# A two-layer hybrid backbone: quadrant sums of FFN weights by accumulating DMA, a plain last FFN part in the first layer, output by tokens

## The chip, the cores and the metric

One NeuronCore of a Trainium2 chip runs the whole program. The metric is device time in microseconds (us), the median of three runs. TensorE is PE in the profile, VectorE DVE, ScalarE ACT, GpSimd POOL, and SP is the engine that issues DMAs.

## What is computed

`x` is 512 latent tokens of width 1024, `ctx` 256 context tokens; all is float32, and there are two layers (`l` = 0 and 1 in the code, "first" and "second layer" here).

```python
hx = modulate(rmsnorm(x, norm1), sh1, sc1)            # shifts, scales, gates from c @ w_mod
... = split_proj(hx @ w_in)                           # 4 head groups: attention, HGRN2, GQA, Fourier
x = x + g1 * (concat(mixers) @ w_out)
x = x + g2 * swiglu(modulate(rmsnorm(x, norm2), sh2, sc2), w_ffn_in, w_ffn_out)
# swiglu(h): gate, up = split(h @ w_ffn_in); (silu(gate) * up) @ w_ffn_out, hidden width 2816
# the context does the same in the first layer only; at the end: rmsnorm(x, final_norm)
```

## The kernel before

**Float32 by halves.** Each float32 operand of a large product is split into two float16 parts, a high one and what is left (`cpo` makes the high part, mostly on ACT; `tto` or `sto` the low part, mostly on DVE), and each product is three matmuls (`PASS`). A weight tile is 128 partitions x 8 x 256.

**Two ways through a tile.** Of the feed-forward network (FFN) a layer has 22 weight tiles of the first product ("I") and 12 of the second ("F": 4 column blocks `p` times 3 parts `c` of the hidden width; the last part, `c` = 2, is shorter: 384 elements where the others have 512). A tile is done plainly, or by Winograd's form of Strassen's scheme (`fast`): the weight and the activations are cut in quadrants, and 7 products replace 8. For the 512 latent tokens that is 84 matmuls of 256 columns instead of 96 (63 instead of 72 in the last part); for the context, 84 of 128 columns instead of 48 of 256. `TUNE['cl']` lists the I tiles that are done plainly: 0, 1, 19 in the first layer, twelve in the second. All F tiles are fast but one, the last of the second layer.

**What a fast tile costs beside PE.** `split_fast` loads the tile in two halves (512 KB each, queue of SP), and makes seven operands of 512 elements a partition: the quadrants A11, A12, A22 and the sums S1 to S4. Each of the seven is a float16 copy with scale (ACT, `L418`) and a low part (DVE, `L434`); each of the four sums is one float32 TENSOR_TENSOR before that (`tto`, `L430`, DVE unless POOL is chosen). S2 is made from S1, S4 from S2. A plain tile has four such element passes over 1024 and no sums (`split_thread`). `pair_ev` puts the gate and up products together out of the seven results, `hid_pair` splits the hidden activations and forms their sums, and `resid_pair` adds a fast F tile's results to the residual (8 DVE instructions for latents, 8 for the context); their plain counterparts are `ffn_ev` and `resid_ffn` (2 DVE instructions for each group of 256 tokens).

**The order of the work** is fixed when the kernel is built: `Plan.run` takes operations from many threads, with a cost for each (`c_dve`, `c_act`, `c_pe`, a landing time `ldma` for a DMA), and appends each to its engine's queue. The queues then run in that order on the chip. Where the plan leaves a gap of over 1.2 us on PE, `fill` puts matmuls on constant data into it (`warm`, `L2466`, 256 columns each); they compute nothing that is used.

**The layer border and the end.** When a group's residual of the last F part is done, `norm_thread` starts: squares, sums over the partitions by a matmul with ones (`L799`), the power -1/2 on POOL (`L817`), a matmul that spreads the result (`L820`), then the modulated activations, which the next layer's first product (`L2054`) needs. At the very end the same thread multiplies the final gain in and writes the output with channels on the partitions; the host transposes it.

Of the kernel before, what the change touches and what calls it, by code (L numbers as in the profile page):

```python
# [2599 lines left out]
```

## Time and profile before

| | us |
|---|---|
| median of 3 runs (1721.33 to 1722.03) | 1721.76 |
| the profiled execution, its own time | 1725.08 |
| its span, first to last instruction | 1723.1 |
| PE busy | 1647.6 |
| DVE busy | 1486.0 |
| ACT busy | 980.8 |
| POOL busy | 150.7 |

The span in stages: input norm and modulation to 95 us, projections and mixers of the first layer to 495, its FFN to 1001, the layer border to 1011, projections and mixers of the second layer to 1321, its FFN to 1708, the final norm to 1723. A matmul's end is modelled and matmuls overlap, so PE busy says where PE stood still, not how fast it ran. Fill matmuls count as busy.

### The profile page before, as it was taken

To read this page: it belongs to the slowest core of one execution; us is meant where nothing else is said; L and a number is where in the kernel's file an instruction comes from. 1 tells how busy PE (TensorE), PEld (TensorE's weight loads), DVE (VectorE), ACT (ScalarE), POOL (GpSimd) and SP (SyncE) were. 2 spreads that over 40 slices of the span, in tenths; PEclk is the share of its full clock that TensorE was granted. 3 is DMA by queue.
4 is the path that set the end of the run, shared out by engine and by line. 5 is a ranking of instruction groups with operands and counts; after the bars stand their busy time and mean duration, and the time that the engine had idled before them with its cause. 6 is when DMAs were issued, how large, how long until landed. Compare 5 with 4: busy or idle time off the path is not lost.

```text
span 1723.1 us, 45511 instructions
## 1 busy us (share of the span) xinstructions
PE 1647.6 (96%) x19493; PEld 1425.4 (83%) x19493; DVE 1486.0 (86%) x3141; ACT 980.8 (57%) x1766; POOL 150.7 (9%) x179
## 2 busy tenths in 40 slices
PE   8999998999999999999999999899889999999998
PEld 5678877887888788898889888788778888888886
DVE  6879899898579897899889998999997788888897
ACT  5637885565465553355435483678955545465454
POOL 0212111230000000000000003430010000000000
PEclk9999999999999999999999999999999999999999
DMA  9822111245045654522352350001113333452631
GB/s 376 326 82 81 57 45 52 71 149 199 38 134 173 199 157 135 161 75 63 118 186 73 122 175 29 14 27 50 51 51 123 136 99 99 137 182 74 194 113 50
DMA packets 62859, 201.40 MB, mean 117 GB/s; under 512 B 6849, under 2 KB 9153, under 8 KB 62657
## 3 DMA queue, kind: packets, MB, share of 16 engines
q1 hardware_dynamic: 62656, 198.50, 35.1%
q8 instruction: 152, 2.49, 0.6%
q14 instruction: 51, 0.41, 0.1%
HBM read 178.55 MB, written 19.92 MB: 115 GB/s over the span
## 4 chain that ended last, share of the span: by engine, by line
PE 52%; DVE 34%; ACT 7%; DMA 4%; issue 2%; POOL 1%; SPq 1%; DVEq 0%; ACTq 0%; POOLq 0%
PE ps L2208 14%; DVE g L430 11%; PE ps L2049 10%; PE ps L2054 6%; DVE g L434 6%; PE ps L2168 5%; DMA g<-xsc 4%; PE ps L616 2%; PE ps L2272 2%; ACT g L418 2%; DVE pl L430 2%; PE ps L1218 2%; ACT g L416 1%; PE ps L1158 1%; PE ps L2466 1%
## 5 line engine op out<-in xcount | busy, mean ns | idle before, releaser
L430 DVE TENSOR_TENSOR g<-g,g 128x512 f32<-128x512 f32 (+7 forms) x698 | 441.0, 659 | 44.8 <-ACT g L416 32.3
L418 ACT ACTIVATE g<-g 128x512 f16<-128x512 f32 (+2 forms) x391 | 242.0, 644 | 236.2 <-DVE g L430 230.4
L2208 PE MATMUL ps<-g,g 128*128 128x256 f16 (+1 forms) x4032 | 361.9, 251 | 1.0 <-DVE g L434 0.8
L2208 PEld LDWEIGHTS <-g 128*128 128x128 f16 x4032 | 326.0, 98 | 40.1 <-issue 11.3
L434 DVE SCALAR_TENSOR_TENSOR g<-g,g 128x512 f16<-128x512 f32 (+4 forms) x442 | 301.1, 697 | 59.1 <-ACT g L418 56.0
L2049 PE MATMUL ps<-g,g 128*128 128x256 f16 x2256 | 271.8, 272 | 2.2 <-DVE g L434 2.0
L2272 PEld LDWEIGHTS <-g 128*128 128x128 f16 x2709 | 225.7, 98 | 43.0 <-issue 14.5
L2049 PEld LDWEIGHTS <-g 128*128 128x128 f16 x2256 | 218.0, 98 | 29.6 <-DVE g L434 2.5
L2272 PE MATMUL ps<-g,g 128*128 128x256 f16 (+1 forms) x1917 | 212.2, 269 | 15.3 <-DVE g L999 4.7
L416 ACT CAST g<-g 128x512 f16<-128x512 f32 (+3 forms) x269 | 162.9, 616 | 76.1 <-DVE g L430 46.6
L2054 PE MATMUL ps<-g,g 128*128 128x256 f16 x1632 | 201.9, 277 | 2.8 <-issue 1.4
L2054 PEld LDWEIGHTS <-g 128*128 128x128 f16 x1632 | 158.5, 99 | 36.8 <-issue 13.9
L2168 PE MATMUL ps<-g,g 128*128 128x256 f16 x1584 | 175.7, 273 | 0.0
L2168 PEld LDWEIGHTS <-g 128*128 128x128 f16 x1584 | 154.7, 98 | 18.9 <-issue 0.8
L416 ACT COPY g<-ps 128x512 f32<-128x512 f32 (+4 forms) x163 | 94.0, 583 | 119.4 <-PE ps L820 24.1
L1198 ACT ACTIVATE g<-ps 128x512 f32<-128x512 f32 x156 | 91.5, 595 | 31.9 <-PE ps L1232 23.1
L430 DVE TENSOR_TENSOR pl<-g,ph 128x512 f16<-128x512 f32 x137 | 93.2, 695 | 7.0 <-ACT ph L416 6.6
L430 DVE TENSOR_TENSOR g<-g 128x256 f32<-128x256 f32 (+3 forms) x197 | 89.4, 462 | 2.4 <-ACT g L754 1.8
L430 POOL TENSOR_TENSOR g<-g,g 128x256 f16<-128x256 f32 (+4 forms) x17 | 23.5, 1386 | 692.0 <-ACT g L416 575.9
L416 ACT CAST ph<-g 128x512 f16<-128x512 f32 (+2 forms) x141 | 80.5, 573 | 4.7 <-DVE g L430 1.0
L1582 ACT ACTIVATE g<-g 128x512 f32<-128x512 f32 x80 | 47.1, 637 | 41.5 <-DVE g L1550 41.3
L1218 PEld LDWEIGHTS <-ph 128*128 128x128 f16 x1248 | 63.3, 97 | 6.5 <-issue 1.7
(248 smaller groups left out, 2207.9 us busy)
## 6 DMA issues: line engine op xcount, KB each, us to landing
g<-in_wall_dram SPq DMA_DIRECT2D x180, 512.0 KB, 4.5
g<-in_wmod_dram SPq DMA_DIRECT2D x96, 512.0 KB, 6.2
g<-xsc SPq DMA_DIRECT2D x40, 256.0 KB, 5.3
xsc<-g SPq DMA_DIRECT2D x40, 256.0 KB, 3.0
g<-in_xg_dram SPq DMA_DIRECT2D x12, 512.0 KB, 6.9
g<-in_wall_dram SPq DMA_DIRECT2D x16, 384.0 KB, 3.3
xsc<-g SPq DMA_DIRECT2D x10, 512.0 KB, 3.1
g<-xsc SPq DMA_DIRECT2D x10, 512.0 KB, 4.5
```

The costliest lines, as they stand in the source:

```text
L416: S.copy(o, i)
L418: S.activation(out=o, in_=i, func=AF.Copy, scale=scale)
L430: return either(r, w, ("dve", c_dve(n), lambda: V.tensor_tensor(**f()), bias, True), ("pool", c_pool(n), lambda: G.tensor_tensor(**f()), 0 ...
L434: return vop(c_dve(n), r, w, lambda: V.scalar_tensor_tensor(**f()), True)
L1198: yield aop(c_act(512), [k], [k + (0,)], lambda pp=pp, bank=bank: S.activation(out=pp, in_=bank, func=AF.Exp, scale=scale), "exp")
L1218: T.matmul(bank[:, u, t, :], lhsT=a[:, i, q], rhs=v[:, b, :], start=(n == 0), stop=(n == 6 * nk - 1))
L1582: yield aop(c_act(512), prev, [k + (r,)], lambda R=R, r=r: S.activation(out=level_view(E, h)[:, :, :, r, :], in_=level_view(R, h)[:, :, :, ...
L2049: T.matmul(bank[:, cb, :], lhsT=W[a][:, kw, 128 * cb:128 * cb + 128], rhs=xh[b][:, kx, :], start=(first and n == 0), stop=(last and n == 2 ...
L2054: T.matmul(bank[:, t, :], lhsT=xh[b][:, k, 128 * t:128 * t + 128], rhs=wt[a][:, k, :], start=(first and n == 0), stop=(last and n == 2), s ...
L2168: T.matmul(bank[:, cb, :], lhsT=wt[a][:, k % 4, :], rhs=xh[b][:, k % 4, :], start=(k == 0 and n == 0), stop=(k == 7 and n == 2), skip_grou ...
L2208: T.matmul(into[name], lhsT=wt[:, y, kk, :], rhs=x[:, z, kk, :], start=(name in ("P1", "P6") and kk == 0 and n == 0), stop=(kk == 3 and n ...
L2272: T.matmul(o, lhsT=wt[:, y, j % 4, :], rhs=x[:, z], start=(name in ("P1", "P6") and j == js[0] and n == 0), stop=(j == js[-1] and n == 2), ...
```

## The change

1. **Sums by DMA.** The FFN weights lie in DRAM by quadrants (`wffn`), and the signs of the scheme are turned so that all four weight sums are additions. S1 and S3 are made by POOL-issued DMAs that add a 256 KB quadrant from DRAM onto one that was loaded (`acc`), two for each fast tile; S2 and S4 stay TENSOR_TENSORs, in place. The plan charges POOL `acp` = 0.9 us for one, lets the sum be there `acl` = 5.2 us later, and adds `accd` = 1.78 us to the DMA queue's clock. Low parts, residual and hidden sums carry the turned sign (`modN`, `-IWS`, subtractions); in `hid_pair` one TENSOR_TENSOR of two rows becomes two of one row.
2. **Which tiles.** First layer: I tile 19 becomes fast, and the four F tiles of `c` = 2 become plain, for latents and context (`PLAIN0`, `hid_pair`, `p_ffn_out`, `out_order`), latents first, group by group. Second layer: nine plain I tiles instead of twelve.
3. **Modulation.** The second layer's 12 modulation loads (2 MB each) begin with tile 16 instead of 14, and one comes with every second weight tile.
4. **Output.** `out_thread` replaces the last norm: PE transposes the gained activations, and the row scale goes in on the way out of PSUM (`L869`), so the output is written by tokens. After the last product, no fill matmuls are placed (`unwarm`).

```diff
-TUNE = {... 'm1': 14, ... 'cl': ((0, 1, 19), (0, 1, 2, 3, 4, 6, 8, 10, 12, 14, 16, 18)), ...}
+TUNE = {... 'm1': 16, ... 'acp': 0.9, 'acl': 5.2, 'gat': 1, 'whq': 16, 'pr_sp': 11, 'rr': 3, 'm1s': 2, 'accd': 1.78, 'p0': 1, 'cord': 0, ... 'cl': ((0, 1), (0, 1, 2, 3, 6, 9, 12, 15, 18)), ...}
@@ Plan.run
-            fin = end + (TUNE["ldma"] if e == "dma" else 0.0)
+            fin = end + (best[2][6] if len(best[2]) > 6 else TUNE["ldma"] if e == "dma" else 0.0)
             eng[e] = end
+            if len(best[2]) > 6:
+                eng["dma"] = max(eng.get("dma", 0.0), start) + TUNE["accd"]
@@ fast
-        return kind == "I" and m not in CL[l] or kind == "F" and (l == 0 or c < 2 or m < TUNE["pc"])
+        return kind == "I" and m not in CL[l] or kind == "F" and (c < 2 or (l == 0 and not PLAIN0) or (l == 1 and m < TUNE["pc"]))
@@ split_fast
-        yield tto(n, ld, [k + (1,)], lambda: dict(out=t, in0=a21, in1=a22, op=ALU.add), TUNE["bws"])
-        yield from put("S1", t, k + (1,))
-        yield tto(n, [("SA", l, i, "S1")], [k + (2,)], lambda: dict(out=t, in0=t, in1=a11, op=ALU.subtract), TUNE["bws"])
...
-        yield tto(n, [ld[0]], [k + (3,)], lambda: dict(out=t3, in0=a11, in1=a21, op=ALU.subtract), TUNE["bws"])
+        def acc(dst, src, rd, key):
+            yield ("op", (("pool", TUNE["acp"], lambda: G.dma_start(dst, src, accum_op=ALU.add), 0.0, False, None, TUNE["acl"]),), rd, [key])
+        def chain():
+            t = R[0][:, 0]
+            yield from put("A11", t, ld[0])
+            yield from acc(t, quad(0, 1), [("SA", l, i, "A11")], k + (3,))
+            yield from put("S3", t, k + (3,))
+            yield from add(t, R[1][:, 1], [("SA", l, i, "S3"), ld[1]], k + (2,))
+            yield from put("S2", t, k + (2,))
+            yield from add(t, R[1][:, 0], [("SA", l, i, "S2"), ld[1]], k + (4,))
+            yield from put("S4", t, k + (4,))
+        def first():
+            t = R[0][:, 1]
+            yield from acc(t, quad(1, 1), [ld[0]], k + (1,))
+            yield from put("S1", t, k + (1,))
@@ hid_pair
+        if l == 0 and j >= 8 and PLAIN0:
+            for u, y in enumerate((a, b)):
...
+                yield cpo(2 * w, kk, [k + (u, "h")], lambda t=t, y=y: (t[:, :, 0], y), ps=False, bias=TUNE["bhh"])
+                yield tto(2 * w, [k + (u, "h")], [k + (u,)], lambda t=t, y=y: dict(out=t[:, :, 1], in0=y, in1=t[:, :, 0], op=ALU.subtract), TUNE["bhl"])
@@ out_order
+        if l == 0 and c == 2 and PLAIN0:
+            for g, p in [(g, p) for g in (1, 2) for p in range(4)] if TUNE["cord"] == 0 else [(g, p) for p in range(4) for g in (1, 2)]:
+                yield "classic", p, (g, c)
+            yield "endx", 0, c
+            for p in range(4):
+                yield "classic", p, (0, c)
@@ out_thread (new; norm_thread loses its last-norm branch)
+        yield gop(0.75, [k + (1,), "zero"], [k + (2,)], lambda: G.tensor_tensor(out=r[:, 1], in0=r[:, 0], in1=nhalf[:, 0:2], op=ALU.pow))
+        os.append((yield from final_gain(g, 3, k)))
+        for h in range(2):
+            for t in range(2):
+                if h:
+                    yield from turn(1, t)
...
+                yield op("dma", c_dma(2048), [kz], [kz + (1,)], lambda z=z, row=row, h=h: nc.sync.dma_start(out[row:row + 128, 512 * h:512 * h + 512], z))
@@ loads
-                    j = TUNE["m1n"] * (i - TUNE["m1"])
-                    for c in range(j, j + TUNE["m1n"]):
-                        if 0 <= c < 12:
-                            load_m(1, mod_order[c])
+                    c, r = divmod(i - TUNE["m1"], TUNE["m1s"])
+                    if r == 0 and 0 <= c < 12:
+                        load_m(1, mod_order[c])
```

Line numbers move: `L430`, `L434`, `L418`, `L2208`, `L2272`, `L2054` and `L2466` before are `L434`, `L438`, `L422`, `L2304`, `L2374`, `L2150` and `L2579` after.

**Place 1: DVE in the second layer's FFN, the sums of one fast tile.** `g` are tiles in SBUF, `ps` banks of PSUM; `L2016`, `L2112`, `L2128` and `L2132` put products together. Before:

```order
L430 TENSOR_TENSOR g_22351<-g_22276,g_22312 128x512
L430 TENSOR_TENSOR g_22362<-g_21939,g_22362 128x2x256
L430 TENSOR_TENSOR g_22006<-g_22006,g_21939 128x256
L434 SCALAR_TENSOR_TENSOR g_22335<-g_22351,g_22335 128x512
L430 TENSOR_TENSOR g_22363<-g_22006,g_22363 128x256
L430 TENSOR_TENSOR g_22351<-g_22351,g_22276 128x512
L434 SCALAR_TENSOR_TENSOR g_22389<-g_22351,g_22389 128x512
L430 TENSOR_TENSOR g_22432<-g_22276 128x512
```

After, the same place:

```order
L438 SCALAR_TENSOR_TENSOR g_22167<-g_22137,g_22167 128x512
L2128 TENSOR_TENSOR g_22086<-g_22085,ps_21976 128x256
L434 TENSOR_TENSOR g_22111<-g_22111,g_22112 128x512
L438 SCALAR_TENSOR_TENSOR g_22167<-g_22137,g_22167 128x512
L2132 TENSOR_TENSOR g_22087<-g_22085,ps_21977 128x256
L438 SCALAR_TENSOR_TENSOR g_22164<-g_22111,g_22164 128x512
L438 SCALAR_TENSOR_TENSOR g_22087<-g_22087,g_22086 128x512
L434 TENSOR_TENSOR g_22111<-g_22111,g_22112 128x512
```

Before, the tile in `g_22276` and `g_22312` has a TENSOR_TENSOR for S1 (`g_22351`), S2 and S3 (`g_22432`) in this piece, and one for S4 later; after, the tile in `g_22111` has two, S2 and S4. And on POOL, where there was no such row:

```order
L906 TENSOR_TENSOR sm_21268<-sm_21268,nhalf 128x2
L517 DMA g_21338<-in_wffn_dram 128x512 x2
L906 TENSOR_TENSOR sm_21553<-sm_21553,nhalf 128x2
L517 DMA g_21496<-in_wffn_dram 128x512 x2
L517 DMA g_22111<-in_wffn_dram 128x512 x2
```

The two accumulating DMAs of a tile (`x2`) stand behind each other, and the second group's power of the norm (`L906`, `L817` before) stands behind a pair.

**Place 2: DVE at the layer border, the residual of the first layer's last context tile.** Before:

```order
L999 TENSOR_TENSOR g_15955<-g_15955,ps_15939 128x256
L430 TENSOR_TENSOR g_15863<-g_15232,g_15788 128x512
L430 TENSOR_TENSOR g_15955<-g_15955 128x128
L1009 TENSOR_TENSOR g_16017<-g_15955,ps_15895 128x128
L1010 SCALAR_TENSOR_TENSOR g_15275<-ps_15895,modG_87,g_15275 128x128
L430 TENSOR_TENSOR g_15835<-g_15877,g_15834 128x512
L1015 SCALAR_TENSOR_TENSOR g_15275<-g_15955,modG_87,g_15275 128x128
L1016 SCALAR_TENSOR_TENSOR g_15275<-g_16017,modG_87,g_15275 128x128
L430 TENSOR_TENSOR g_15964<-g_15231,g_15805 128x512
L1020 TENSOR_TENSOR g_16017<-g_15955,ps_15939 128x128
L1021 SCALAR_TENSOR_TENSOR g_15275<-g_16017,modG_87,g_15275 128x128
```

After:

```order
L434 TENSOR_TENSOR g_15749<-g_15158,g_15679 128x512
L434 TENSOR_TENSOR g_15744<-g_15744,g_15767 128x512
L1065 SCALAR_TENSOR_TENSOR g_15160<-ps_15637,modG_87,g_15160 128x256 x2
L438 SCALAR_TENSOR_TENSOR g_15745<-g_15338,g_15337 128x1024
L434 TENSOR_TENSOR g_15689<-g_15749,g_15688 128x512
L434 TENSOR_TENSOR g_15810<-g_15158,g_15679 128x512
L434 TENSOR_TENSOR g_15744<-g_15744,g_15830 128x512
L1065 SCALAR_TENSOR_TENSOR g_15160<-ps_15697,modG_87,g_15160 128x256 x2
```

Eight residual rows of a context tile (`L999` to `L1021`) have become two (`L1065 x2`), and the 128x512 rows of the latents' norm stand closer together. On PE, 70 fill matmuls stand between the last context product and the second layer's first product before (`L799` and `L2054` follow them); after, `L2150` follows `L2337`, the plain context product, with no fill between.

**Place 3: PE at the end.** Before, behind 27 fill matmuls:

```order
L2466 MATMUL ps_26323<-p16c 128x256
L820 MATMUL ps_26223<-g_26304,p32c 128x256
```

After:

```order
L831 MATMUL ps_25822<-p32c,g_25903 128x1 x2
L842 MATMUL ps_25939<-p32c,g_25813 128x128 x2
L842 MATMUL ps_25939<-p32c,g_25912 128x128 x2
L842 MATMUL ps_25951<-p32c,g_25813 128x128 x2
L842 MATMUL ps_25951<-p32c,g_25912 128x128 x2
L842 MATMUL ps_25962<-p32c,g_25803 128x128 x2
L842 MATMUL ps_25962<-p32c,g_25934 128x128 x2
```

The matmul that spread the row scale (`L820`) is gone; transposes (`L842`, 32 in all, 16 of them before the last sum) stand in its place.

## Rows read from the trace of the kernel before

**Rows 1.** The page: engines over the span, and the chain that ended last, by engine.

```profile
PE 1647.6 (96%) x19493; PEld 1425.4 (83%) x19493; DVE 1486.0 (86%) x3141; ACT 980.8 (57%) x1766; POOL 150.7 (9%) x179
PE 52%; DVE 34%; ACT 7%; DMA 4%; issue 2%; POOL 1%; SPq 1%; DVEq 0%; ACTq 0%; POOLq 0%
```

**Rows 2.** Stages: stretch, its us, busy PE, PEld, DVE, ACT, POOL; clock, DMA share, GB/s.

```profile
495.00:1001.20 506.20, 496.75 (x5740) 439.67 (x5738) 449.01 (x1002) 249.44 (x539) 3.54 (x4) 1.00 0.43 136
1001.20:1011.40 10.20, 8.81 (x83) 7.71 (x80) 10.16 (x23) 9.18 (x17) 0.00 (x0) 1.00 0.43 141
...
1321.00:1668.00 347.00, 342.60 (x3125) 305.67 (x3124) 292.44 (x530) 183.91 (x322) 4.47 (x5) 1.00 0.41 128
1668.00:1688.30 20.30, 16.90 (x132) 13.20 (x129) 18.21 (x40) 10.30 (x23) 0.00 (x0) 0.92 0.01 3
...
1708.00:1723.10 15.10, 7.45 (x48) 5.71 (x46) 7.20 (x15) 2.17 (x5) 1.41 (x2) 0.75 0.40 139
```

**Rows 3.** The same stages, fill matmuls (L2466) alone: PE, PEld.

```profile
495.00:1001.20 506.20, 5.79 (x47) 4.48 (x47) 1.00 0.43 136
...
1321.00:1668.00 347.00, 4.75 (x39) 3.81 (x39) 1.00 0.41 128
1668.00:1688.30 20.30, 6.81 (x47) 5.19 (x47) 0.92 0.01 3
```

**Rows 4.** Timeline: runs of matmuls; start, us, engine, line, shapes, count.

```profile
997.02 0.33 PE L2272 MATMUL ps<-pl,g 128*128 128x128 f16 x3
997.18 0.50 PE L2272 MATMUL ps<-ph,g 128*128 128x128 f16 x6
...
1654.74 13.37 PE L2208 MATMUL ps<-g,g 128*128 128x256 f16 x121
```

**Rows 5.** Timeline at the layer border: fills, DVE's norm work, the next layer's start.

```profile
1001.33 7.81 PE L2466 MATMUL ps<-p16c 128*128 128x256 f16 x70
...
1004.27 4.90 DVE L430 TENSOR_TENSOR g<-g,g 128x512 f16<-128x512 f32 x8
...
1011.56 0.38 PE L2054 MATMUL ps<-g,g 128*128 128x256 f16 x2
```

**Rows 6.** DVE by form, 495 to 1001 us: busy, mean ns of one | idle before, releaser.

```profile
L434 DVE SCALAR_TENSOR_TENSOR g<-g,g 128x512 f16<-128x512 f32 x189 | 127.7, 688 | 32.2 <-ACT g L418 31.7
L430 DVE TENSOR_TENSOR g<-g,g 128x512 f32<-128x512 f32 x113 | 77.2, 686 | 0.7 <-ACT g L416 0.3
...
L434 DVE SCALAR_TENSOR_TENSOR g<-g,g 128x384 f16<-128x384 f32 x28 | 14.9, 554 | 2.4 <-ACT g L418 2.3
...
L1010 DVE SCALAR_TENSOR_TENSOR g<-ps,modG,g 128x256 f32<-128x256 f32 x12 | 5.8, 481 | 4.0 <-DMA g<-xsc 4.0
...
L1010 DVE SCALAR_TENSOR_TENSOR g<-ps,modG,g 128x128 f32<-128x128 f32 x11 | 3.8, 347 | 0.3 <-DMA g<-xsc 0.3
...
L423 DVE CAST g<-g 128x512 f16<-128x512 f32 x7 | 3.0, 423 | 0.6 <-ACT g L416 0.5
```

**Rows 7.** Timeline of the last 15 us.

```profile
1708.06 0.88 DVE L983 SCALAR_TENSOR_TENSOR g<-ps,modG,g 128x256 f32<-128x256 f32 x2 [1.29 <-PE ps L2235]
...
1711.06 0.70 POOL L817 TENSOR_TENSOR sm<-sm,nhalf 128x2 f32<-128x2 f32 x1 [1.26 <-DVE sm L816]
...
1715.77 0.60 PE L820 MATMUL ps<-g,p32c 128*128 128x256 f32 x2
...
1716.81 2.50 DVE L430 TENSOR_TENSOR g<-g,g 128x512 f32<-128x512 f32 x4 [2.21 <-ACT g L416]
```

**Rows 8.** DMA issues: kind, count, KB each, median us from issue to landing.

```profile
g<-in_wall_dram SPq DMA_DIRECT2D x180, 512.0 KB, 4.5
```

**Rows 9.** Residual loads (L954, 256 KB each, on SP): all from issue to landing.

```profile
DMA to landing us min/median/max: 3.2/5.3/8.3
```

**Rows 10.** Output stores (L829, 256 KB each, on SP): the same.

```profile
DMA to landing us min/median/max: 2.2/2.4/2.6
```

More of the change, by code (lines that the diff above doesn't have):

```diff
@@ L52 @@
 W_OUT0 = 11
+W_FFN0 = 15
 def _order():
@@ L336, with kernel @@
 @with_exitstack
-def kernel(ctx: ExitStack, tc: tile.TileContext, xg, wall, wmod, pk32, pk16, dftx, dftc, out):
+def kernel(ctx: ExitStack, tc: tile.TileContext, xg, wall, wffn, wmod, pk32, pk16, dftx, dftc, out):
     nc = tc.nc
@@ L368 @@
     modG = [const.tile([128, 2, 2, 8], F32, name=f"modG{l}") for l in range(NL)]
+    modN = [const.tile([128, 2, 8], F32, name=f"modN{l}") for l in range(NL)]
     lamt = const.tile([128, NL], F32, name="lamt")
@@ L498, in split_fast, with quad @@
         users = 2 if l == 0 else 1
[L499 to L506 removed]
+        A = st["A", l, i] = {}
+        R = [None, None]
+        left = [2, 2]
+        def quad(h, q):
+            return wffn[l, i - W_FFN0, :, h, q, 0:nr, :]
         def put(name, src, key):
[L509 removed]
+            yield wait(("pk", l, i, name))
             dst = A[name][:, :, 0:nr]
@@ new lines, in over, with add @@
+        def over(h):
+            left[h] -= 1
+            if not left[h]:
+                plan.free(R[h])
+        def add(dst, src, rd, key):
+            yield tto(n, rd, [key], lambda: dict(out=dst, in0=dst, in1=src, op=ALU.add), TUNE["bws"])
+        def chain():
+            t = R[0][:, 0]
+            k = ("SS", l, i)
+            yield from put("A11", t, ld[0])
+            yield from acc(t, quad(0, 1), [("SA", l, i, "A11")], k + (3,))
+            yield from put("S3", t, k + (3,))
+            yield wait(ld[1])
+            R[1] = st["ld", ("w", l, i), 1]
+            yield from add(t, R[1][:, 1], [("SA", l, i, "S3"), ld[1]], k + (2,))
+            yield from put("S2", t, k + (2,))
+            yield from add(t, R[1][:, 0], [("SA", l, i, "S2"), ld[1]], k + (4,))
+            over(1)
+            yield from put("S4", t, k + (4,))
+            over(0)
@@ new lines, in first, with other @@
+        def first():
+            t = R[0][:, 1]
+            k = ("SS", l, i)
+            yield from acc(t, quad(1, 1), [ld[0]], k + (1,))
+            yield from put("S1", t, k + (1,))
+            over(0)
+        def other():
+            yield from put("A12", R[1][:, 0], ld[1])
+            yield from put("A22", R[1][:, 1], ld[1])
+            over(1)
+        yield wait(ld[0])
+        R[0] = st["ld", ("w", l, i), 0]
+        plan.spawn(first(), TUNE["pr_sp"])
+        plan.spawn(chain(), TUNE["pr_sp"])
@@ new lines, in split_fast @@
+        for u, ab in enumerate(PACK):
+            if u == 1 and TUNE["gat"]:
+                yield wait(("SS", l, i, 3))
+            if u == 2:
+                yield wait(ld[1])
+                R[1] = st["ld", ("w", l, i), 1]
+                plan.spawn(other(), TUNE["pr_sp"])
+            t = yield alloc("g", [128, 2, 2, 4, 128], F16, w_reserve, ("wh", TUNE["whq"]))
+            for v, name in enumerate(ab):
+                A[name] = t[:, v]
+                st["WT", l, i, name] = t
+                plan.done["pk", l, i, name] = (0.0, "none")
+            uses[id(t)] = users * len(ab)
@@ L672, in fG @@
                     V.tensor_scalar(out=modG[l][:, w, v, 4 * half:4 * half + 4], in0=modv[l][:, 4 * c:4 * c + 4, v], scalar1=IWS, scalar2=None, op0=ALU.mult)
+                    if w:
+                        V.tensor_scalar(out=modN[l][:, v, 4 * half:4 * half + 4], in0=modv[l][:, 4 * c:4 * c + 4, v], scalar1=-IWS, scalar2=None, op0=ALU.mult)
             yield vop(0.2, [("mod", l, c)], [("modG", l, w, half)], fG)
@@ L2382, in out_order, with unwarm @@
             yield "endc", 0, c
+    def unwarm():
+        plan.warm = None
     def prod_thread():
```

195 lines of the change are left out of this document (111 added, 84 removed).

## The prediction

> **What bounds the kernel now.** I read the page's first part and the chain that ended last [rows 1]: PE is busy for 96% of the span, yet only 52% of the chain runs on PE and 34% on DVE. So PE is the long pole, and DVE is what it waits for when it waits. The stages show where [rows 2]. In the first layer's FFN PE stands still for 506.2 - 496.75 = 9.5 us while DVE is busy for 449 of 506 us (89%). At the layer border PE does nothing useful for 10.2 us: its 8.81 busy us are fill matmuls [rows 5], DVE is busy all of that time (10.16), and its last long run there is eight TENSOR_TENSORs of the norm, up to 1009 us, before the second layer's first product at 1011.56. In the second layer's FFN PE stands still for 4.4 us up to 1668 and for 3.4 us in the 20 us after it, where DVE is busy for 18.2 of 20.3. To idle PE belongs what fill matmuls hide [rows 3]: 5.8 us in the first layer's FFN, 4.75 and 6.8 us in the second's. After the last product come 15.1 us of norm and stores.
>
> So four pools of PE time can be won: 9.5 + 5.8 = 15.3 us, 10.2 us, 4.4 + 4.75 + 3.4 + 6.8 = 19.4 us, and part of the 15.1. What lies in the projections and mixers the change hardly touches.
>
> **DVE work, part by part.** A fast tile loses two of its four sums: 2 x 0.686 [rows 6] = 1.37 us. In the first layer 27 tiles stay fast: -37 us. The four F tiles that become plain lose, each, four sums and seven low parts of 384 elements (11 x 0.554 = 6.1 us) against two low parts of 768 (about 0.95 each, by the step of 0.134 us from 384 to 512 elements: 1.9); the latents' residual goes from eight instructions of 0.42 to 0.69 us (3.9 us) to four of the size of L1010's 0.481 (1.9), the context's from eight of about 0.33 (2.7 us; L1010's 128x128 takes 0.347) to two (1.0). That is 4.2 + 2.0 + 1.7 = 7.9 us a tile, 32 in all; the six plain hidden splits (three pairs, latents and context) have two low parts instead of five and no sums, about 2.4 us less each by the same forms, 14 more. I tile 19 becomes fast: some 7 us more. The divided TENSOR_TENSOR of `hid_pair` adds some 0.15 us for each of 16 pairs, 2 us. Sum for the first layer's FFN: -37 - 46 + 7 + 2 = -74 us out of 449. In the second layer 21 tiles stay fast (-28 us) and three become fast (5.5 us each, +17 with the hidden sums): about -10 us.
>
> **PE work.** A matmul of 256 columns takes 13.37 / 121 = 0.1105 us, one of 128 columns (0.50 - 0.33) / 3 = 0.056 [rows 4]. First layer: four latent F tiles get 72 instead of 63 wide matmuls (+36); for the context 36 wide ones replace 63 narrow ones (+18 wide in effect); tile 19 gives back 12 and 6. Net +36, or **+4.0 us**. Second layer: three tiles x 12 wide matmuls less, **-4.0 us**.
>
> **Layer border, -8.7 us.** Of the 74 us that DVE loses, 46 lie in the last F part and its context tail. The latents' norms now start group by group, the first while the second group's 144 products run, and the context's 144 products (144 x 0.1105 = 15.9 us) come last as cover for the rest. I leave 1.5 of the 10.2 us for the start. The 70 fills have gone from the order.
>
> **First layer's FFN, -8.8 us beside the +4.0.** With DVE at some 375 of 500 us (75%), most waits end. The order still has 31 fills (3.4 us) and I leave 3 us of other waits: 6.4 of 15.2 remain.
>
> **Second layer's FFN, -10.9 us beside the -4.0.** DVE's load falls little, but ordered fills fall from 86 to 32, and at the end, where DVE is the chain, the last fast tiles each lose two sums. I leave 3.5 us for fills and 5 us of waits: 8.5 of 19.4.
>
> **The end, -5.6 us.** Now: residual 0.88 us, square, sum, power 0.70, spread matmul (L820, 0.60 with the transfer out of PSUM behind it), then four multiplications in 2.50 us, the second group's behind the first's on DVE, then stores [rows 7]. After: no spread matmul, copy or diagonal; half the transposes are done before the last sum; two scalings of the last group go to ACT and two to DVE, so that 2.5 us become about 1.3. With the same chain to the power (over at 1711.8), two rounds of 0.6 to 0.7 us and the same 3.8 us from the last scaling to the span's end, it ends at 1717.5 instead of 1723.1. The fills behind the last product ran in a wait anyway; without them nothing is lost but PE's clock, and few matmuls are left to feel it.
>
> **Accumulating DMAs, +4 us.** The trace has none. Below, one can't be quicker than the quickest row of its size: 2.2 us, a 256 KB store [rows 10]. Above, it is a slowest load and a slowest store after one another, 8.3 + 2.6 = 10.9 us [rows 9, 10]. I take 6, near the median load of 256 KB (5.3) with something for the second read; the plan's allowance is 0.9 + 5.2 = 6.1. By the Trainium skill, "DMA: Bandwidth & Descriptors", section "Anatomy of one DMA", a POOL-issued transfer takes about 2.0 us and bytes / 436 GB/s, 2.6 us for 256 KB, an estimate for a plain copy; by that this term would be 0 and the sum 4 us lower, and no run here shows it. Behind a late sum stand, on POOL, the tile's other accumulation and one power of a norm; on ACT, its float16 copies and whatever copy out of PSUM follows; on DVE, low parts and the residual; on SP, the next load into the same buffer. 104 issues at the plan's 0.9 us are 94 us of a POOL that was busy for 151 of 1723 [rows 1]: no bound. They add some 27 MB of reads to DMA engines that are busy 41 to 43% there [rows 2]. An early sum gives nothing by itself, as the queues are fixed, so the term lies between 0 and the 53 us worked out below. The 4 us are for the first tile of each FFN, whose sums nothing covers, and for stragglers.
>
> **The rest.** Fifteen more fills stand in the second layer's mixers (38 against 23): +1.7 us. The spread modulation loads cost nothing as long as the last, at tile 38 of 49, lands before the layer border; if that cover went, the border would wait for a load of 512 KB, 4.5 us [rows 8]. Sign changes and `modN` (eight tiny instructions): nothing.
>
> **Sum.** -8.7 - 8.8 + 4.0 - 10.9 - 4.0 - 5.6 + 4.0 + 1.7 = -28.3 us. The profiled execution took 1725.08 us (span 1723.1 and 2.0 around it), 3.3 above the median; so 1696.8 as profiled, and 1721.8 - 28.3 = **1693.5** as a median.
>
> **The rivals.**
> *Sums that come too late (slower).* The queues are fixed, so DVE's spare time is all that absorbs lateness, once for each tile, as its two sums are issued together. Spare per fast tile: in the first layer (57 + 74) / 28 = 4.7 us, in the second (55 + 10) / 24 = 2.7. If every sum is later than the plan's 6.1 us by d, the cost is 28 (d - 4.7) + 24 (d - 2.7), each where positive; it eats the gain of 28 at d = 3.9, that is at 10.0 us from issue to sum. At the upper bound of 10.9, d = 4.8 gives 3 + 50 = 53, and 1721.8 - 28.3 + 53 = 1746. For it: a fixed order, and loads that often take 5 us and up to 8.3. Against: it needs each sum near the worst case, and the DMA engines are half idle. DVE casts that run beside POOL are few, seven of 0.42 us in the first FFN [rows 6], so a POOL held up by each would be late by no more than that. The Trainium skill, "SBUF — State Buffer", section "Who interferes with whom", speaks against the change here: a DVE cast or copy in its two-port mode locks POOL out of SBUF for the whole instruction, and POOL writes its descriptors there. By that rule the chance would be above 0.1; the row shows too few such casts for that. From the rows I give the case 0.08.
> *The waits are not DVE's load.* If the FFN waits come from landing times, PSUM and the in-order queues, both FFN pools stay; only border, end, PE and the small terms count: -8.7 + 4.0 - 4.0 - 5.6 + 4.0 + 1.7 = -8.6, 1713. For it: much of DVE's idle time is a wait for ACT's copy (32 us [rows 6]), which stays. 0.12.
> *Everything closes.* No waits left in either FFN or at the border, sums always early: -10.2 - 15.2 + 4.0 - 19.4 - 4.0 - 5.6 + 1.7 = -48.7, 1673. 0.10.
> *The change does nothing in sum:* lateness just eats the gain (d near 3.9). 0.04.
>
> **How the numbers follow.** My forecast gets 0.66. Faster by over 0.2% (3.4 us, about what a measurement of this kernel can tell from no change): 0.66 + 0.12 + 0.10 = 0.88; within: 0.04; slower: 0.08. The lower end of the range is the forecast with the sums free (-4) and three quarters of the waits that I left (1.5 + 6.4 + 8.5 = 16.4, so -12.5) gone too: 1677. The upper end takes in the second rival and 3 us of lateness on it: 1716. Left out are the slower case, the flat one and most of the third: 0.08 + 0.04 + 0.08.
>
> **What the profile after would show.** DVE busy near 1400 us; fills 218; PE without a break over 2 us at the border; 104 POOL DMAs of 256 KB that land within about 6 us; the end within 10 us of the last product. I am wrong if sums land at 10 us or more and ACT's copies (L422) wait for DMA, if PE's idle time in the FFNs stays above 25 us with DVE well under 85%, or if the border still holds PE for 5 us or more.

## The result, and the profile after

The changed kernel takes 1736.11 us (median of 5, 1730.71 to 1737.36) where the kernel before takes 1722.03 beside it: ratio 1.006, 95% interval 1.004 to 1.008. It is slower by 0.6% (0.8% by the two medians alone); the prediction said 1693.5 us, faster. The profiled execution took 1730.82 us, with a span of 1729.0, near the lower end of its runs.

The page of the changed kernel, engines and chain by engine [rows 1]:

```profile
PE 1634.3 (95%) x19285; PEld 1412.4 (82%) x19285; DVE 1413.2 (82%) x3023; ACT 960.6 (56%) x1729; POOL 237.7 (14%) x282
...
PE 56%; DVE 21%; DMA 10%; issue 7%; ACT 5%; POOL 1%; SPq 0%; ACTq 0%; POOLq 0%; DVEq 0%
```

DVE lost 73 us of work, near the forecast (1413 against some 1400), and its share of the chain fell from 34% to 21%. DMA rose from 4% to 10%, issue from 2% to 7%.

The stages [rows 2, same columns], cut where PE begins each FFN, the second layer's mixers and the last norm; first before, then after:

```profile
495.20:1011.50 516.30, 505.47 (x5818) 447.30 (x5816) 459.07 (x1024) 258.55 (x555) 3.54 (x4) 1.00 0.43 136
1011.50:1368.00 356.50, 334.83 (x4452) 293.30 (x4453) 315.05 (x650) 238.62 (x375) 62.20 (x73) 0.99 0.19 62
1368.00:1708.00 340.00, 332.52 (x3010) 294.85 (x3009) 294.88 (x552) 180.13 (x336) 1.75 (x2) 0.99 0.38 117
```

```profile
488.00:1016.60 528.60, 510.58 (x5722) 445.55 (x5720) 405.21 (x910) 245.59 (x513) 50.45 (x59) 0.99 0.61 173
1016.60:1374.60 358.00, 337.50 (x4479) 296.35 (x4478) 309.77 (x648) 234.00 (x374) 62.95 (x75) 0.99 0.18 60
1374.60:1717.00 342.40, 324.35 (x2917) 287.05 (x2914) 284.13 (x552) 178.04 (x345) 42.57 (x49) 0.98 0.57 151
1717.00:1729.00 12.00, 5.20 (x49) 4.96 (x47) 4.12 (x10) 4.54 (x8) 1.45 (x2) 0.82 0.47 175
```

In the two FFNs PE stands still for 18.0 us each (528.60 - 510.58; 342.40 - 324.35), against 10.8 and 7.5 before, although DVE is now busy for only 77% of the first and 83% of the second. The first FFN starts 7.2 us earlier and is over 5.1 us later. Of the 7.2 us, 3.9 are modulation matmuls (`L649`) that moved into it; the rest lies in a stretch that the change hardly touches, at a granted clock of 1.00 instead of 0.98. The DMA engines are busy for 61% and 57% instead of 43% and 38%.

What arrives late, from the waits of all engines (engine, line and tile, who is waited for; us in total, times, longest; `xsc` holds the residual), and the accumulating DMAs from issue to landing:

```profile
ACT g L422 <- DMA g<-in_wffn_dram: 104.1, 52, 6.4
...
DVE g L1092 <- DMA g<-xsc: 19.4, 6, 6.0
```

```profile
DMA to landing us min/median/max: 3.5/6.6/10.1
```

ACT's float16 copies stand 104 us for a weight quadrant; by the trace's releasers 93 of these are for a sum and 11 for a plain load of the same tensor. The plan counted on it 0.9 + 5.2 = 6.1 us after issue; the median is 6.6, and 59 of the 104 land later than planned, by 94 us in all (landing minus 6.1 for each, where positive, added up from the trace).

One such wait for a sum, in the timeline of the second layer's FFN:

```profile
1573.59 1.73 POOL L517 DMA_DIRECT2D g<-in_wffn_dram  x2 [17.34 <-ACT g L420]
...
1576.73 2.57 PE L2304 MATMUL ps<-g,g 128*128 128x256 f16 x22
...
1581.25 0.63 ACT L422 ACTIVATE g<-g 128x512 f16<-128x512 f32 x1 [4.98 <-DMA g<-in_wffn_dram]
1581.79 0.37 ACT L2129 ACTIVATE g<-ps 128x256 f32<-128x256 f32 x1
1581.92 0.69 DVE L438 SCALAR_TENSOR_TENSOR g<-g,g 128x512 f16<-128x512 f32 x1 [4.36 <-ACT g L422]
...
1585.02 0.57 ACT L420 COPY g<-ps 128x512 f32<-128x512 f32 x1
...
1585.64 2.72 PE L2304 MATMUL ps<-g,g 128*128 128x256 f16 x12 [6.34 <-ACT g L420]
```

The sum lands 7.64 us after its issue. ACT is idle for 4.98 us before the copy that needs it, DVE for 4.36 behind ACT; the copy out of PSUM that would free a bank for PE (`L420 COPY`) stands further back in ACT's queue, and PE waits 6.34 us for it, far more than the 1.5 us by which this sum missed its plan. Of the ten breaks of over 1.2 us in the FFNs (1.8 to 6.3 us), six lie in the stretches with F products (`L2374`), where residual loads share the DMA engines with weights and sums; four, this one among them, lie between I products.

Two signs came out as forecast. At the border PE goes from the context's last products (`L2337`) to the second layer's first (`L2150`) without a break or a fill [rows 5]:

```profile
1015.43 0.82 PE L2337 MATMUL ps<-pl,g 128*128 128x256 f16 x6
1016.09 0.82 PE L2337 MATMUL ps<-ph,g 128*128 128x256 f16 x6
1016.74 1.47 PE L2150 MATMUL ps<-g,g 128*128 128x256 f16 x12
```

And fills are 218 in all. The end is 12.0 us long, not 9.5.

### The profile page after: what moved, and what is told of

Read it like the earlier page. It is cut to its first block, busy times and chain, and to the rows that moved or that the text cites. A ratio compares the mean times of both kernels' runs of the same rounds, so it can differ in the third digit from the quotient of the medians.

```text
span 1729.0 us, 45274 instructions
## 1 busy us (share of the span) xinstructions
PE 1634.3 (95%) x19285; PEld 1412.4 (82%) x19285; DVE 1413.2 (82%) x3023; ACT 960.6 (56%) x1729; POOL 237.7 (14%) x282
## 3 DMA queue, kind: packets, MB, share of 16 engines
q0 software_dynamic: 14976, 26.88, 9.4%
## 4 chain that ended last, share of the span: by engine, by line
PE 56%; DVE 21%; DMA 10%; issue 7%; ACT 5%; POOL 1%; SPq 0%; ACTq 0%; POOLq 0%; DVEq 0%
PE ps L2304 12%; PE ps L2145 10%; DMA g<-in_wffn_dram 8%; PE ps L2374 7%; PE ps L2150 6%; DVE g L434 5%; PE ps L2264 4%; PE ps L2337 3%; DVE g L438 3%; PE ps L649 2%; PE ps L1300 2%; DVE pl L434 2%; DMA g<-in_wmod_dram 1%; PE ps L1240 1%; DVE g L1630 1%
## 5 line engine op out<-in xcount | busy, mean ns | idle before, releaser
L434 DVE TENSOR_TENSOR g<-g,g 128x512 f32<-128x512 f32 (+8 forms) x639 | 392.5, 641 | 54.7 <-ACT g L420 40.9
L2304 PE MATMUL ps<-g,g 128*128 128x256 f16 (+1 forms) x4452 | 409.5, 254 | 16.2 <-ACT g L420 6.3
L2304 PEld LDWEIGHTS <-g 128*128 128x128 f16 x4452 | 366.0, 98 | 65.3 <-issue 24.1
L422 ACT ACTIVATE g<-g 128x512 f16<-128x512 f32 (+3 forms) x390 | 241.8, 649 | 222.3 <-DMA g<-in_wffn_dram 104.1
L438 DVE SCALAR_TENSOR_TENSOR g<-g,g 128x512 f16<-128x512 f32 (+5 forms) x450 | 305.9, 703 | 63.5 <-ACT g L422 60.6
L2145 PE MATMUL ps<-g,g 128*128 128x256 f16 x2256 | 271.8, 273 | 2.2 <-DVE g L438 2.0
L2145 PEld LDWEIGHTS <-g 128*128 128x128 f16 x2256 | 218.1, 98 | 29.5 <-DVE g L438 2.5
L2374 PEld LDWEIGHTS <-g 128*128 128x128 f16 x2205 | 189.5, 99 | 37.7 <-issue 19.9
L2150 PE MATMUL ps<-g,g 128*128 128x256 f16 x1632 | 196.8, 273 | 2.5 <-issue 1.2
L2374 PE MATMUL ps<-g,g 128*128 128x256 f16 (+1 forms) x1629 | 178.6, 271 | 16.2 <-DVE g L1081 11.1
L420 ACT CAST g<-g 128x512 f16<-128x512 f32 (+2 forms) x251 | 154.4, 622 | 68.8 <-DVE g L434 40.8
L517 POOL DMA_DIRECT2D g<-in_wffn_dram x104 | 89.9, 947 | 686.3 <-ACT g L422 149.0
L2150 PEld LDWEIGHTS <-g 128*128 128x128 f16 x1632 | 156.1, 98 | 34.0 <-issue 12.9
L420 ACT COPY g<-ps 128x512 f32<-128x512 f32 (+4 forms) x155 | 90.1, 588 | 142.5 <-PE ps L909 27.8
L2264 PE MATMUL ps<-g,g 128*128 128x256 f16 x1152 | 127.7, 273 | 2.1 <-DVE g L434 2.1
L2264 PEld LDWEIGHTS <-g 128*128 128x128 f16 x1152 | 112.7, 98 | 15.6 <-DVE g L434 2.3
L434 DVE TENSOR_TENSOR pl<-g,ph 128x512 f16<-128x512 f32 x137 | 92.9, 694 | 3.7 <-ACT ph L420 3.3
L420 ACT CAST ph<-g 128x512 f16<-128x512 f32 (+2 forms) x133 | 77.0, 581 | 4.7 <-DVE g L434 1.6
L1242 DVE TENSOR_REDUCE sm<-ps 128x2 f32<-128x512 f32 x104 | 64.7, 680 | 3.0 <-PE ps L1240 2.7
```

Of the source, the lines that this page charges most:

```text
L420: S.copy(o, i)
L422: S.activation(out=o, in_=i, func=AF.Copy, scale=scale)
L434: return either(r, w, ("dve", c_dve(n), lambda: V.tensor_tensor(**f()), bias, True), ("pool", c_pool(n), lambda: G.tensor_tensor(**f()), 0 ...
L438: return vop(c_dve(n), r, w, lambda: V.scalar_tensor_tensor(**f()), True)
L517: yield ("op", (("pool", TUNE["acp"], lambda: G.dma_start(dst, src, accum_op=ALU.add), 0.0, False, None, TUNE["acl"]),), rd, [key])
L2145: T.matmul(bank[:, cb, :], lhsT=W[a][:, kw, 128 * cb:128 * cb + 128], rhs=xh[b][:, kx, :], start=(first and n == 0), stop=(last and n == 2 ...
```

## The experiments

The diffs below show only the part of a line that changes; buffer bookkeeping is left out. "Late in sum" is worked out as above, against the planned instant of each kernel. e1, e2, e5 and e15 leave out the sums, in whole or in part, and only serve to take the time apart. e1 to e4, e5 to e8, e9 to e12 and e13 to e16 ran on one chip each, with the kernel before beside them (medians 1722.7 to 1725.6), so runs of different groups are compared by ratio; 0.001 is 1.7 us, and a difference of two ratios is uncertain by 0.002 to 0.004, 4 to 6 us.

| run | us | ratio, interval | late in sum, us |
|---|---|---|---|
| changed kernel | 1736.1 | 1.006, 1.004 to 1.008 | 94 |
| e1 small sums | 1695.7 | 0.983, 0.982 to 0.985 | 4.5 |
| e2 plain copies | 1705.9 | 0.988, 0.986 to 0.990 | 10 |
| e3 sums by TENSOR_TENSOR | 1713.9 | 0.994, 0.992 to 0.996 | |
| e4 modulation as before | 1735.5 | 1.006, 1.005 to 1.008 | 79 |
| e5 small sums, adding onto spare tiles | 1721.0 | 0.999, 0.997 to 1.000 | 45 |
| e6 sums planned later | 1706.3 | 0.991, 0.988 to 0.994 | 3.4 |
| e7 one sum by DMA | 1726.3 | 1.002, 1.001 to 1.004 | 17 |
| e8 e3 without plain part | 1717.2 | 0.997, 0.996 to 0.999 | |
| e9 sums planned earlier | 1745.7 | 1.013, 1.011 to 1.016 | 166 |
| e10 loads and sums planned later | 1697.5 | 0.986, 0.983 to 0.988 | 38 |
| e11 the same, sums later still | 1702.5 | 0.989, 0.986 to 0.991 | 7 |
| e12 e3, loads planned later | 1699.3 | 0.987, 0.984 to 0.989 | |
| e13 kernel before, loads planned later | 1717.2 | 0.996, 0.994 to 0.997 | |
| e14 loads alone planned later | 1716.1 | 0.996, 0.994 to 0.997 | 88 |
| e15 e6 with small sums | 1696.4 | 0.984, 0.982 to 0.986 | 0.7 |
| e16 e7, loads planned later | 1702.6 | 0.988, 0.986 to 0.989 | 17 |

### The same order, less in the DMA: e1 and e2

```diff
-lambda: G.dma_start(dst, src, accum_op=ALU.add)
+lambda: G.dma_start(dst[:, 0, 0:32], src[:, 0, 0:32], accum_op=ALU.add)    # e1
+lambda: G.dma_start(dst, src)                                             # e2
```

> The changed kernel with its queues in the same order, but each accumulating DMA adds only 16 KB (128 x 32) of the 256 KB quadrant; the rest of the sum is left out. Theory L (the sums land late, and the in-order ACT and DVE queues pass that on to PE): sums land in under 4 us instead of 6.6, ACT's waits on them (104 us) fall below 30, PE's breaks that the trace leads back to a sum go (2.4 + 3.7 + 1.3 + 2.2 + 6.5 + 5.2 = 21 us), 1710. Theory C (26 MB more on the DMA engines delay every other transfer, the residual round trips above all): those too (10 us), 1700, with the residual loads back at a median of 5.3 us from 7.0. Theory O (the order itself holds the waits: spread modulation, fewer DVE sums in other places): within 5 us of 1736.

> The changed kernel with its queues in the same order, but the POOL-issued DMAs of 256 KB copy the quadrant over the loaded one instead of adding to it; the additions are left out. If the adding is what makes them slow (a read and a write of SBUF for each element): they land near the plain loads (5 us or less) and the time falls to 1710 to 1720. If it is the traffic and the queue: landing stays over 6 us, time within 5 us of 1736.

Measured: 1695.7 and 1705.9. The order of every queue is that of the changed kernel, so the order alone doesn't cost the time: theory O falls. e1 is below what either L or C asked for, so it doesn't choose between them; ACT's wait (`L422`) falls to 44 us, not below 30. From issue to landing, e1 and then e2:

```profile
DMA to landing us min/median/max: 2.2/3.6/8.1
```

```profile
DMA to landing us min/median/max: 2.9/4.3/8.1
```

The same 256 KB land 2.3 us sooner by the median as a plain copy than when they are added. The DMA queue's line (packets, MB, share of 16 engines' span) of the changed kernel and of e2 shows what the adding takes from the DMA engines:

```profile
q0 software_dynamic: 14976, 26.88, 9.4%
```

```profile
q0 software_dynamic: 8224, 26.88, 5.1%
```

For the same 26.88 MB the adding takes 144 packets a DMA instead of 79, and 0.094 x 1729 = 163 us of all 16 engines instead of 0.051 x 1705 = 87. The FFN stages of e1, in which PE stands still for 7.8 and 4.2 us, and the second layer's mixers between them:

```profile
487.50:997.50 510.00, 502.25 (x5722) 442.00 (x5721) 406.42 (x910) 245.20 (x513) 50.36 (x59) 1.00 0.50 152
997.50:1356.50 359.00, 338.06 (x4480) 295.62 (x4479) 310.70 (x648) 234.37 (x374) 62.77 (x75) 0.99 0.18 59
1356.50:1681.40 324.90, 320.71 (x2916) 285.73 (x2915) 283.28 (x551) 178.00 (x345) 42.58 (x49) 0.99 0.42 125
```

The sums' DMAs thus cost 0.023 of the time (1.006 - 0.983), 39 us. The two FFNs account for it: they are 36 us shorter in e1, 24 of them PE's standstill and 12 its busy time.

Between e1 and e2, at the same order, lie 0.005, 9 us, with little lateness in either. That would be traffic if nothing else differed, but the same stages of e2 place only part of it where the sums run:

```profile
489.50:1004.70 515.20, 506.02 (x5723) 444.07 (x5721) 405.86 (x910) 245.56 (x513) 32.81 (x59) 0.99 0.55 177
1004.70:1367.50 362.80, 342.16 (x4480) 300.03 (x4478) 309.57 (x647) 233.96 (x374) 62.57 (x75) 0.97 0.18 59
1367.50:1691.10 323.60, 320.26 (x2916) 285.65 (x2914) 283.32 (x551) 177.87 (x345) 27.46 (x49) 0.99 0.49 160
```

The FFNs are longer by 515.20 + 323.60 - 510.00 - 324.90 = 3.9 us. Another 3.8 us lie in the mixers, where POOL issues a single sum, at a granted clock of 0.97 instead of 0.99. The residual loads' median went from 7.0 us to 6.2 in e1, not to the 5.3 that theory C asked for.

### Undoing parts: e3, e4, e7, e8

```diff
# e3: both sums by TENSOR_TENSOR (e7: S1 alone, read straight after both loads)
-yield from acc(t, quad(0, 1), [("SA", l, i, "A11")], k + (3,))
+yield from add(t, R[0][:, 1], [("SA", l, i, "A11"), ld[0]], k + (3,))
-yield from acc(t, quad(1, 1), [ld[0]], k + (1,))
+yield from add(t, R[1][:, 1], [k + (3,), ld[1]], k + (1,))
# e4
-'m1': 16, 'm1s': 2
+'m1': 14, 'm1s': 1
# e8: e3 and
-'p0': 1
+'p0': 0
```

> The changed kernel with S1 and S3 made by TENSOR_TENSOR again, in place, all else (plain last part, spread modulation, new output, nine plain tiles) kept. DVE +71 us of work (104 x 0.69), fill matmuls in the order 342 instead of 218 (+13.7 us of PE by the plan). Theory L or C: the FFNs lose their unplanned breaks (31 us) and pay the planned ones; border and end keep their gain: 1715 to 1722. Theory O: breaks stay and DVE's work comes on top, 1745 or more.

> The changed kernel with the second layer's modulation loaded as before (from tile 14, one with each tile). Fills 269 instead of 218 (+5.6 us, by the plan). Theory C: the first layer's FFN has 12 x 2 MB less beside the sums, its breaks behind residual loads (2.8 + 2.0 + 2.0 + 2.6 = 9 us) go, 1727 to 1732. Theory L: the sums are late all the same, within 4 us of 1736 or slower by the fills.

> The changed kernel with S3 by accumulating DMA and S1 by TENSOR_TENSOR (52 accumulating DMAs instead of 104); 275 fills. If both sums cost alike, it lies midway between both by DMA and both by TENSOR_TENSOR, (1736 + 1714) / 2 = 1725. If the serial chain A11, S3, S2, S4 is what can't bear lateness: 1732 or more. If the DMA engines' load is what counts, it falls with its square or so: 1718 or less.

> All four sums by TENSOR_TENSOR as in the third experiment (1714), and the last part of the first layer's FFN by Strassen's form again. By the prediction's terms the plain part is worth its share of the border (8.7 us) and of DVE's 46 us there less 4.0 us of PE; fills 387 instead of 342 (+5 us): 1722 to 1728. If the plain part is worth nothing: 1714 or less.

e3, 1713.9, beats both kernels: without the accumulating DMAs the rest of the change gains 0.0065, 11 us. It pays for its sums in DVE work (1471 us busy) and 342 ordered fills. e4 moves nothing: the spread modulation is not the cause. One sum by DMA instead of two (e7) lies between e3 and the changed kernel. At 1726 it seems midway, as expected if both cost alike; by ratio it is 0.0089 above e3 and 0.0036 below the changed kernel, so one sum costs more than half of what two do, though its sums are late by 17 us in all instead of 94. e8 is 0.0036, 6 us, slower than e3: the plain last part is worth about that, less than its terms gave (8 to 14).

### Traffic without a wait: e5

```diff
+G.dma_start(dst[:, 0, 0:32], src[:, 0, 0:32], accum_op=ALU.add)
+G.dma_start(spare[turns[0] % 2][:, 0:nr], src, accum_op=ALU.add)
```

> The changed kernel with its queues in the same order; each sum is again the 16 KB addition of the first experiment (the rest of the sum is left out), but behind it POOL issues the whole 256 KB accumulating DMA onto a spare tile that nothing reads. So the traffic of the adding is there and no engine waits for it. If the loss is lateness of the sums themselves: within 6 us of the 1696 with small sums. If it is what the adding takes from the DMA engines (other loads and round trips late): 1720 to 1736, with the residual loads at a median of 7 us.

Measured 1721.0, and it doesn't tell: the small sums landed at a median of 5.1 us instead of 3.6, 45 us late in sum, so lateness was not taken away. A tile's second small sum is issued behind its first large one.

### What the plan counts on: e6, e9, e15

```diff
-'acl': 5.2
+'acl': 7.6    # e6; e9: 3.4; e15: 7.6 and the 16 KB sums of e1
```

> The changed kernel built with acl 7.6 instead of 5.2, so that the plan counts on a sum 8.5 us after its issue instead of 6.1 (landing on the chip: median 6.6, nine in ten under 8.6); 258 fills in the order instead of 218 (+4.4 us). If the loss comes from sums that miss the planned time and from queues in an order that can't bend: most of the 30 us come back, 1705 to 1715. If it comes from contention, whatever the order: 1730 or more.

> The changed kernel built with acl 3.4 instead of 5.2: the plan counts on a sum 4.3 us after its issue, where the chip takes 6.6 by the median; 262 fills in the order instead of 218 (+4.8 us). So far the time follows the lateness past the planned instant, added up over the 104 sums: 94 us late in the changed kernel, 10 with plain copies, 4.5 with small sums, 3.4 with the later plan, at about 0.3 to 0.45 us of time for each us. If that holds, this one is 200 to 240 us late in sum and takes 1770 to 1800. If lateness is not what counts, it stays within 10 us of 1736.

> The sixth experiment (acl 7.6, 1706) with its queues in the same order, each accumulating DMA cut to 16 KB (the rest of the sum is left out). Sums are late by 3 us in all there, so lateness plays no part in the difference. If the adding also costs time by its traffic (other transfers late): 1690 to 1698. If lateness was all: 1703 to 1707.

e6 does the same work, with 40 more fills, and issues the same DMAs, which land nearly as before (median 6.1, up to 9.6), and takes 1706 us. Its three stages and ACT's wait:

```profile
486.80:1005.90 519.10, 508.00 (x5765) 446.45 (x5764) 405.79 (x907) 246.62 (x515) 50.74 (x60) 1.00 0.63 176
1005.90:1368.80 362.90, 343.06 (x4480) 300.79 (x4478) 309.21 (x647) 234.06 (x374) 62.88 (x75) 0.97 0.18 59
1368.80:1690.60 321.80, 319.19 (x2915) 284.76 (x2912) 283.43 (x549) 180.24 (x347) 41.90 (x49) 1.00 0.61 161
```

```profile
ACT g L422 <- DMA g<-in_wffn_dram: 43.6, 33, 6.2
```

The DMA share is as high as in the changed kernel (0.63 and 0.61), PE's standstill 11.1 and 2.6 us instead of 18.0 twice. e15, with e6's order and hardly any bytes, is 0.0073, 13 us, faster than e6. Here too only part lies where the sums run: of 8.8 us between the two profiled executions, 3.1 are in the FFNs (840.9 against 837.8) and 5.0 in the mixers (362.9 us at 0.97 against 357.9 at 0.99).

So the same adding, landing nearly alike, costs 39 us against small sums at the recorded plan, and 13 at the later one. **Traffic costs at most 9 to 13 us** (e2 against e1, e15 against e6), 3 to 4 by the FFN stages alone; whether the mixers' lower clock is its work no run shows. **Sums past their planned instant cost the rest, 26 us or more**, found by subtraction.

e9 is slower by 0.0074, 13 us, not by 35 to 65: lateness in sum nearly doubles (166 us), yet each further microsecond costs less than the first. As written, its 1745.7 is within 10 us of 1736, the branch in which lateness counts for nothing; only the ratios set it apart.

### What the plan counts on for loads: e10 to e14, e16

```diff
-'acl': 5.2, 'ldma': 1.8
+'acl': 6.4, 'ldma': 4.0    # e10; e11: 7.6 and 4.0; e14: 5.2 and 4.0
# e12, e13, e16: 'ldma': 4.0 in e3, in the kernel before, and in e7
```

> The changed kernel built with ldma 4.0 instead of 1.8 (every load from SP counted on later) and acl 6.4 (sums 7.3 us after issue); 218 fills as in the changed kernel. Theory L: sums late by some 30 us in all instead of 94, so 40 % of 64 = 25 us less, and the residual loads' waits (10 us) fall too: 1698 to 1712. Without effect of the plan's allowances: 1730 or more.

> As the one before, with acl 7.6 (sums 8.5 us after issue); 280 fills (+6.8 us). Theory L: nearly no lateness left (under 10 us in sum), but more planned gaps: 1700 to 1710, against 1706 with ldma 1.8. If the residual loads are the rest of the loss: under 1700.

> All four sums by TENSOR_TENSOR (third experiment, 1714), built with ldma 4.0; 341 fills instead of 342. If the allowance for loads helps by itself, whatever makes the sums: 1704 to 1710. If only the accumulating DMAs need it: 1714 within 4 us, and the gain of the two runs before is theirs.

> The kernel before, built with ldma 4.0 instead of 1.8 and nothing else; fills 437 in the order instead of 370 (+7.4 us). If a truer allowance for loads helps any version of this kernel: 1708 to 1715. If the kernel before had no loss from late loads (its FFN waits were DVE's): 1722 to 1730, and the gain of ldma 4.0 belongs to the changed versions.

> The changed kernel built with ldma 4.0 and acl left at 5.2 (sums planned 6.1 us after issue, as on record); 228 fills instead of 218 (+1.1 us). If the sums' lateness is the larger part of the loss: 1718 to 1728. If the loads' allowance is all that matters: within 5 us of the 1697 that both allowances gave together.

> S3 alone by accumulating DMA, S1 by TENSOR_TENSOR (the seventh experiment, 1726), built with ldma 4.0; 266 fills instead of 275. Between both sums by DMA with both allowances (1697) and both by TENSOR_TENSOR (1699), if what costs is only what the plan doesn't know: 1695 to 1702. If a sum that misses 6.1 us by a few costs as before: 1710 or more.

The plan lets every load from SP be there 1.8 us after its issue ends; on the chip 512 KB take 4.5 us [rows 8]. With 4.0 the changed kernel gains 18 us (e14), with the sums' allowance too 35 (e10, 1697.5, the fastest version that computes everything). Its FFN stages:

```profile
490.80:1000.40 509.60, 500.16 (x5732) 441.89 (x5731) 409.00 (x914) 241.74 (x507) 52.90 (x61) 1.00 0.63 179
...
1358.30:1682.00 323.70, 319.84 (x2908) 285.10 (x2906) 283.38 (x551) 179.68 (x345) 42.20 (x49) 0.99 0.61 160
```

They are as short as those of e1. That leaves little room for traffic. The kernel before gains 7 us (e13), e3 gains 12 (e12, 1699.3), e7 25 (e16); e12 and e14 came out 5 and 2 us below their ranges, e13 2 above. e10 and e12 can't be told apart: once the plan's times fit, two sums by DMA are worth no more than two by TENSOR_TENSOR. Why e12 gains is open. ACT's float16 copies waited only 6.7 us for DMA in e3, and ordered fills are 341 against 342; but PE's standstill in the FFNs falls from 13.3 us to 4.2. So part of what the allowances do may be that another order falls out better, and e14 (88 us late in sum, 1716) and e16 against e7 (both 17) show that lateness in sum alone doesn't give the time. The 39 and the 13 us each rest on pairs of the same order and don't hang on this.

## Why the prediction was wrong

Point by point, by its own steps; e1 shows each term without the sums' weight.

- **First FFN and border** (-8.8, +4.0, -8.7): in e1 the second layer's mixers begin at 997.5 instead of 1011.5, -14.0 against -13.5. Right in size, with some luck: 7.7 of it lie before the FFN, and the moved modulation matmuls explain 4.4 of these; the other 3.3 lie in the stretch whose granted clock differs (0.99 against 0.98). The border is closed in the changed kernel too. DVE's loss in this stretch was overrated (459.1 to 405.2, -54 instead of -74), but PE's waits closed without it. Of the missing 20 us, 12 are a matter of reading: added up instruction by instruction DVE loses 66 us (528.5 to 462.6), but neighbours overlap in the trace, so busy time falls by less than means times counts. The other 8 stay open.
- **Second mixers** (+1.7): 358.0 instead of 356.5 in the changed kernel, +1.5. Right.
- **Second FFN** (-10.9, -4.0): 340.0 to 324.9 in e1, -15.1 against -14.9. Right; in the changed kernel +2.4.
- **The end** (-5.6): 15.1 to 12.0, -3.1. What was missed are the column sums of the last group, which stand behind the transposes on PE, and a longer way through the stores (5.7 us from the last scaling's end to the span's, not 3.8); the power ends 4.6 us after the last product, not 3.8:

```profile
1717.10 0.87 DVE L1065 SCALAR_TENSOR_TENSOR g<-ps,modG,g 128x256 f32<-128x256 f32 x2 [1.75 <-PE ps L2337]
...
1718.98 1.07 PE L842 MATMUL ps<-p32c,g 128*128 128x128 f32 x8
1719.89 0.50 PE L831 MATMUL ps<-p32c,g 128*128 128x1 f32 x4
...
1720.89 0.73 POOL L860 TENSOR_TENSOR sm<-sm,nhalf 128x2 f32<-128x2 f32 x1 [0.93 <-DVE sm L858]
1720.93 2.42 ACT L869 ACTIVATE g<-ps,sm 128x512 f32<-128x512 f32 x4 [0.24 <-PE ps L842]
```

- **Accumulating DMAs** (+4): this is the step that failed. Their landing was taken as 6 and is 6.6 by the median, so the duration was close; what it costs was not. Measured: 39 us, by e1. Without it the change gains 0.017, 29 us, against 32.3 in the other terms.

The fault lies in the formula "the cost is 28 (d - 4.7) + 24 (d - 2.7)", which made the first rival decide at 10.0 us from issue to sum. It let DVE's spare time of a whole stage absorb each tile's lateness, and it used one d for all. But the copy that waits is on ACT, and behind it in the same queue are the copies that free PSUM for PE. DVE's spare time lies elsewhere and can't be spent there. By the formula a d of 0.5 costs nothing. Sums that were 0.5 us late by the median, with nine in ten under 8.6 us, cost 26 us or more. The timeline above shows that way for one sum; that all of the cost goes through ACT's queue is not shown. The second part of the miss, traffic, I set to nothing with "the DMA engines are half idle". It is the smaller part: an adding DMA costs them nearly twice a plain one, and residual loads went from a median of 5.3 us [rows 9] to 7.0, of which small sums take back 0.8.

The first rival was thus the right mechanism, with a wrong price and so a wrong chance of 0.08. Its page's rule, that a DVE cast in two-port mode locks POOL out of SBUF for the whole instruction (the Trainium skill, "SBUF — State Buffer", section "Who interferes with whom"), had no part that the trace shows: the 104 issues took 847, 859 and 1206 ns (minimum, median, maximum), and of the 29 over 1000 ns 28 overlap no cast or copy on DVE. The estimate of 2.6 us by the Trainium skill, "DMA: Bandwidth & Descriptors", section "Anatomy of one DMA", was for a plain copy; e2 measures 4.3 for it among the other transfers, and the adding takes 6.6: the measurement decides. Of the conditions under which I said I would be wrong, one was met: PE's idle time in the FFNs is 36 us with DVE at 77% and 83%. Of another only half was: ACT's copies wait for DMA, but the sums land at 6.6 us by the median and not at 10.

## What to carry to other kernels

Where queues are ordered ahead, the time that the plan allows a transfer is part of the kernel: measure its landing under load and allow for the late ones (here 8.5 us, near the ninetieth percentile, took the cost of the adding from 39 us to 13), since a sum late by a microsecond or two can hold all that stands behind it on an in-order queue. Such a plan changes the order too: the allowance for loads alone moved versions without sums by DMA by 7 and 12 us (e13, e12). And with the plan mended, two sums by DMA were worth no more than two on DVE. Idle time of one engine is no reserve for a wait on another; ask what stands behind the waiting instruction. Price a DMA that adds at twice a plain copy's share of the DMA engines before it takes work from an engine.

## What was unexpected of the hardware

- An accumulating DMA of 256 KB takes 144 packets and about 1.9 times the DMA engines' time of a plain copy (163 against 87 us for 104 of them, six of which are 192 KB), lands in 6.6 against 4.3 us by the median, and holds POOL for 947 ns by the mean against 545.
- A break can cost PE more than itself. Around the wait of 6.34 us shown above, by stretches of 10 us (same columns as the stages), the mean granted clock falls to 0.57, between its levels of 1.2 and 2.4 GHz, and is 0.92 in the next stretch, in which PE is busy throughout; before the break it was 1.00, with PE busy for 9.3 of 10 us:

```profile
1570.00:1580.00 10.00, 9.30 (x86) 8.19 (x84) 6.98 (x15) 3.60 (x8) 3.47 (x4) 1.00 0.58 139
1580.00:1590.00 10.00, 4.36 (x21) 3.04 (x21) 8.08 (x16) 6.75 (x14) 0.00 (x0) 0.57 0.53 126
1590.00:1600.00 10.00, 10.00 (x87) 8.61 (x86) 8.77 (x18) 6.03 (x12) 1.68 (x2) 0.92 0.53 160
```

  With the same matmuls in the same order PE is busy for 834.9 us of the two FFNs in the changed kernel (510.58 + 324.35) and for 823.0 in e1, at granted clocks of 0.99 and 0.98 instead of 1.00 and 0.99: up to 12 us of the loss are matmuls that take longer. Not all of this follows late sums: over its whole span e2, with few breaks, is at 0.987, as low as the changed kernel (0.988).
